# Background sums spaced otherwise, five ordinary tiles ahead of the seven-product groups, and relu with its transposes one step back

## The chip, the cores and the metric

The kernel runs on one core of a Trainium2 chip. The time is device microseconds of one execution, lower is better; what is compared is the median of several executions. The engines are named as the profile names them: PE is TensorE (matmul), PEld its weight load, DVE is VectorE, ACT is ScalarE, POOL is GpSimd, and SP is SyncE, which only issues transfers here. Each engine takes its instructions in the order in which they were written; an instruction that waits holds up all that is queued behind it on its engine.

## The reference

One decoder layer on 256 tokens of width 2048, all in float32:

```
h = rmsnorm(x);  proj = h @ w_in                      # 2048 x 4160
a_out = dilated sliding-window attention, 8 heads     # on the first 3072 columns
b_out = latent attention, 8 heads                     # w_uq, w_ukv
x = x + rmsnorm(concat(a_out, b_out) @ w_out)
h = rmsnorm(x)
u = square(relu(h @ w_up))                            # 2048 x 8192
x = x + rmsnorm(u @ w_down)                           # 8192 x 2048
```

The change lies in the product with `w_up` (the up product), and in transfers that prepare it in the background.

## The kernel before

Stages run one after another: the product with `w_in` and the first attention (to about 190 us of the profiled execution), the latent attention (to about 260), the product with `w_out` (to about 374), the up product (374 to 742), the product with `w_down` (to the end). Weights come as tiles of 128 rows by 1024 columns (512 KB). SP issues the load of a tile into one of five `raw` buffers; ACT rounds it to a first part `hi` (line 308, or 312 where the norm's gain is multiplied in), DVE takes the rest `lo` (line 309 or 313), each into one of eight buffers that are free again when PE has used the tile. A product is then three matmuls of 128x512: hi by hi, lo by hi, hi by lo.

The up product has eight chunks j of 1024 columns. A chunk holds four 128x512 accumulators, for two halves of the tokens and two halves of the columns: half the banks of PSUM, in turn. It walks over sixteen rows of tiles k in two ways. An *ordinary tile* ("k") takes twelve matmuls. A *group* ("w") covers two rows k at once by seven products of half blocks in place of eight, 21 matmuls instead of 24, with sums of weight blocks (right sums) and sums of token blocks (left sums). Three of its products and four others use the four middle banks `m`, which are those that the chunk before has emptied. At a chunk's end the four m banks are combined by ACT and DVE into four tiles c (`close`, lines 1090 and 1093), and DVE adds them onto the accumulators (line 1163). Then the chunk's result leaves: four times ACT makes `r` from an accumulator by relu (line 965), PE transposes r in four pieces into the same bank (`rt`, line 302), and ACT squares that into `uT` (line 978). These steps are spread over the next chunk's first tiles. The next chunk's first group cannot start before the last of them, as it takes those banks for its m.

The right sums of a group come in two ways. *Inline*: POOL fetches two weight tiles into `ab` or `ab2` (line 399), DVE makes the sums t and u (lines 386, 390, 391), and ACT and DVE split them. *Made*: for twelve groups (the table `MADE`), POOL issues transfers from DRAM to DRAM long before (line 368): one copies the two tiles (1024 KB), two add weight blocks onto the copy (512 KB and 256 KB), one adds a block of the copy onto others (512 KB). Each waits for those before it on the same group. They go in batches of `MADE_BATCH` groups: the batch's copies, then its additions, then its last additions.

The order in which each engine's instructions are written comes from a list of steps (`UP_STEPS`) and from chains with a clock of their own (the class `Flow`): each matmul written adds its modelled time to the clock, and a chain's next step is written when the clock has reached its due time. `make_sums` is such a chain: it begins at `D_MADE` and writes one transfer every `MADE_STEP`. `up_evac` is another: `UP_STEP * order` (2.2 each) after it was started it writes the relu, 1.8 later the transposes and the square. These times set only the order of writing. How long something takes on the chip is set by waits.

Of the kernel before, what the change touches and what calls it, by code (L numbers as in the profile page):

```python
# [96 lines left out]


MADE = [(), (1,)] + [(1, 3)] * 5 + [(1,)]
D_MADE, MADE_STEP, MADE_BATCH = 62.0, 4.8, 3  # L100


def up_steps(first, *groups):
    steps = [("k", k) for k in first]
    for i, ks in enumerate(groups):
        steps += [("w", i)] + [("k", k) for k in ks]
    return steps
# [1 line left out]

THREE = up_steps(range(6, 11), (11, 12), (13,), (14, 15))  # L110
FOUR = up_steps(range(8, 12), (12,), (13,), (14,), (15,))
FIVE = up_steps(range(10, 14), (), (14,), (), (), (15,))
UP_STEPS = [up_steps(range(16)), THREE] + [FIVE] * 5 + [FOUR]

ST = 12 * 256
N_SEVEN = [sum(w == "w" for w, _ in steps) for steps in UP_STEPS]
# [149 lines left out]
def layer(nc, tc, io):  # L266
    flow = Flow()
# [12 lines left out]
    def bank(i, name):  # L280
        return ps.tile([P, 512], F32, tag=f"bank{i}", bufs=1, name=name)
# [19 lines left out]
    def transpose(out, a):  # L301
        nc.tensor.transpose(out, a, ident)
        flow.spend(TR)
# [182 lines left out]
    def proj(aT, chs, name, order=None, need=None, bank_of=None):  # L486

        accs = [[[(bank_of or acc_bank)(f"acc_{name}_{c}_{b}_{i}") for i in range(len(ch.cuts))] for b in range(NB)]
                for c, ch in enumerate(chs)]
        order = order or [(0, t, b) for t, b in in_order(len(chs[0].tiles))]  # L490
        left = {(c, b): len(ch.tiles) for c, ch in enumerate(chs) for b in range(NB)}
        uses = {}
        for c, t, b in order:
            ch = chs[c]
            i, k0, kp = ch.tiles[t]
            ws = [weights.get(x) for x in (i if isinstance(i, list) else [i])]
            i = i if isinstance(i, list) else [i]
            if need:
                need(k0 + kp - 1, b)
            if i[0] < FINE:  # L500
                hl = [(0, 0), (1, 0)], [(0, 1)]
            else:
                hl = [(0, 0), (0, 1), (1, 0)],
            for g, passes in enumerate(hl):
                for kk in range(kp):
                    k = k0 + kk
                    for j, (o, m) in enumerate(ch.cuts):
                        wt, o = (ws[j], 0) if len(ws) > 1 else (ws[0], o)
                        for p, (x, w) in enumerate(passes):
                            mm(accs[c][b][j][:, :m], tok(aT[x], k, b), wt[w][:, kk, o:o + m],  # L510
                               k == 0 and g == 0 and p == 0,
                               k == ch.nk - 1 and g == len(hl) - 1 and p == len(passes) - 1, MM * m / 512)
                    flow.pump()
            left[c, b] -= 1
            for x in i:
                uses[x] = uses.get(x, 0) + 1
                if uses[x] == NB:
                    weights.free(x)
            if not left[c, b]:
                yield c, b, accs[c][b]  # L520
# [188 lines left out]
    for half in range(2):  # L709
        qkv = {}  # L710
        for nms in (("qk", "v") if not half else "qkv"):
            accs = [acc for _, _, acc in proj(xT, [ch_a[half, nms]], f"{nms}{half}",
                                              bank_of=at_bank if (half, nms) == (0, "v") else None)]
# [217 lines left out]
    for ns in ((0, 1), (2,), (3,)):  # L931
# [4 lines left out]
        for c, b, acc in proj(mixT, [ch_o[n] for n in ns], f"o{ns[0]}", order, heads_done):  # L936
            n = ns[c]
# [23 lines left out]
    def up_evac(j, b, i, acc, order):  # L961

        yield UP_STEP * order
        r = late["up"].tile([P, 512], F32, tag="r", bufs=2, name=f"r{j}_{b}")
        nc.scalar.activation(r, acc, AF.Relu, scale=rstd2[b])
        yield D_UP if j > 1 else 2 * D_UP
        t = bank(i, f"rt{j}_{b}")
        for k in range(4):
            transpose(t[:, k * P:(k + 1) * P], r[:, k * P:(k + 1) * P])
        if j not in uT:  # L970
            if j < 2:
                t2 = late["u01"][:, j * CW:(j + 1) * CW]
            elif j > 13:
                t2 = late["up"].tile([P, CW], F32, tag="T", bufs=2, name=f"uT{j}")
            else:
                t2 = late["up"].tile([P, CW], F32, tag=f"k{U_HOME.get(j, j)}", bufs=1, name=f"uT{j}")
            uT[j] = t2.rearrange("p (k s) -> p k s", k=4)
        nc.scalar.activation(uT[j][:, :, b * P:(b + 1) * P], t.rearrange("p (k s) -> p k s", k=4), AF.Square)
        if b and 2 <= j < 8:
            flow.start(u_away(j), 6.0)  # L980
# [119 lines left out]
    evac = []  # L1100
    for j in range(FF // CW):
        at = {bn: 4 * (j % 2) + i for i, bn in enumerate(PARTS)}
        if j == 0:
            accs = {bn: acc_bank(f"acc_u0_{bn[0]}{bn[1]}") for bn in at}
            at = {bn: (turn[0] - 3 + i) % 4 for i, bn in enumerate(at)}
        else:
            accs = {bn: bank(i, f"acc_u{j}_{bn[0]}{bn[1]}") for bn, i in at.items()}
        steps = wide_u[j]
        order = in_order(len(steps), (APART[1], 0)) if j == 0 else [(t, b) for t, (w, _, _) in enumerate(steps)
                                                                    for b in range(NB if w == "k" else 1)]  # L1110
        for t, b in order:
            what, k, tiles = steps[t]
            if (j, t, b) == (0, 8, 0):
                flow.finish(*res)
                late["po"].release()
                mix.release()
                late["up"] = pool("up", "right")
                late["st"] = late["up"].tile([P, ST], F32R, tag="st", bufs=1, name="st")
                late["st4"] = late["up"].tile([P, CW], F32R, tag="k2", bufs=1, name="st4")
                for n in ("ab", "ab2", "c", "u01"):  # L1120
                    late[n] = late["up"].tile([P, 2 * CW], F32, name=n)
                flow.start(all_sums())
            if (j, t, b) == (FF // CW - 1, 4, 0):
                weights.limit -= 1
                u_next = split_u(0, 0)
            if (j, what, k, b) == (1, "k", 10, 0):
                more_sums = flow.start(two_sums(), 12.0)
            if (j, what, k) == (1, "w", 2):
                flow.finish(more_sums)
            if (j, t, b) == (FF // CW - 1, 6, 0):  # L1130
                for i in (2, 3):
                    u_back(i, late["up"].tile([P, CW], F32, tag=f"k{i}", bufs=1, name=f"uT{i}_back"))
            if j == 1 and what == "w":
                flow.until(lambda: len(sums) > k)
            if what == "k":
                w = weights.get(tiles[0])
                h_done(k, b)
                for n in range(2):
                    c = slice(n * 512, (n + 1) * 512)
                    three(accs[b, n], [tok(hT[x], k, b) for x in range(2)], [w[x][:, 0, c] for x in range(2)], t == 0, t == len(steps) - 1)  # L1140
                    if j == 0 and t == len(steps) - 1:
                        evac.append(flow.start(up_evac(n, b, at[b, n], accs[b, n], 2 * b + n - 0.25 * (2 * b + n))))
                    flow.pump()
                if b == NB - 1:
                    weights.free(tiles[0])
                continue

            first, last = k == 0, k == N_SEVEN[j] - 1
            if first:
                weights.ahead = W_AHEAD  # L1150
                flow.finish(*evac[-4:])
                m = {n: bank(i, f"m{n}_{j}") for n, i in zip((1, 6, 7, 5), free)}
            blocks = [[tok(hT[x], 2 * k + kk, bb) for x in range(2)] for kk, bb in ((0, 0), (1, 0), (1, 1))]
            if last:
                weights.ahead -= 1
            seven_products(tiles, (blocks, sums[k]), accs, m, first, last, last and N_SEVEN[j] > 3, k in MADE[j])
            if last:
                more = close(closing(), m)
        free = [at[bn] for bn in PARTS]
        if j:  # L1160

            for bn in PARTS:
                nc.vector.tensor_tensor(out=accs[bn], in0=accs[bn], in1=more[bn], op=OP.add)  # L1163
            for o, (b, n) in enumerate(PARTS):
                evac.append(flow.start(up_evac(2 * j + n, b, at[b, n], accs[b, n], o + 0.6)))
    weights.ahead = W_AHEAD
    u_last = evac[-4:]
    up = late["up"]
# [84 lines left out]
    for c in range(2):  # L1253
# [3 lines left out]
        accs = {(b, n): y[b][2 * c + n] for b, n in PARTS}  # L1257
# [107 lines left out]
```

## Time and profile before

| what | us |
|---|---|
| three executions | 1086.21, 1086.35, 1082.34 |
| median | 1086.21 |
| the profiled execution's own time | 1084.39 |
| span of the profiled execution | 1082.6 |
| PE busy in the span | 1042.8 (96%) |
| DVE busy in the span | 836.4 (77%) |
| 16 DMA engines, moved | 273.39 MB, 253 GB/s on the mean |
| mean granted TensorE clock | 0.992 of full speed |

Times inside the profile count from the span's start. A matmul's time in the records overlaps with that of the next one (about 390 ns each, begun about 227 ns apart), so PE's busy share says little by itself; gaps in PE and what ended them say more. Chunks 2 to 6 of the up product, from 470 to 694 us, repeat with a period of 44.6 us, so that one of them stands for five.

### The profile page before, as it was taken

The page shows a single profiled execution, that of the slowest core. Times are in us where ns is not written, and L with a number is a line of the kernel's source. Part 1 is how long each engine was busy: PE and PEld are TensorE (multiplying, and loading weights), DVE is VectorE, ACT ScalarE, POOL GpSimd, SP SyncE. Part 2 cuts the span into 40 slices and gives each one's busy share as a digit, 9 for nine tenths or more (in the row PEclk, how much of TensorE's full clock was granted, in tenths as well). Part 3 has the DMA queues.
Part 4 walks back from the last instruction along what each step waited for, and adds up shares of the span by engine and source line. Part 5 has one row for each costly group of instructions (what it writes and reads, how often), then busy time and mean ns, then how long its engine had stood idle before and what let it go on. Part 6 is the DMA issues. An engine that isn't in the chain of part 4 may idle for free.

```text
span 1082.6 us, 13538 instructions
## 1 busy us (share of the span) xinstructions
PE 1042.8 (96%) x4819; PEld 862.3 (80%) x4819; DVE 836.4 (77%) x1122; ACT 636.5 (59%) x862; POOL 96.0 (9%) x128
## 2 busy tenths in 40 slices
PE   9997899999999999999999999998999999999996
PEld 6886789888788878878778787787888888888885
DVE  6664446566556569889899898897799988999995
ACT  6564345655355466566657557576566655766761
POOL 0022100232101010000000000000000000111100
PEclk9999999999999999999999999999999999999999
DMA  8989967999929476668668585659778767789962
GB/s 299 355 286 259 314 178 227 236 276 323 269 97 302 159 269 246 216 202 280 218 230 273 186 282 190 219 201 390 250 253 293 284 241 263 271 286 315 372 206 85
DMA packets 96692, 273.39 MB, mean 253 GB/s; under 512 B 8304, under 2 KB 12912, under 8 KB 96240
## 3 DMA queue, kind: packets, MB, share of 16 engines
q1 hardware_dynamic: 70624, 190.35, 51.1%
q0 software_dynamic: 25568, 81.80, 25.4%
q8 instruction: 38, 0.62, 0.2%
q10 hardware_dynamic: 432, 0.37, 0.1%
q14 instruction: 30, 0.25, 0.1%
HBM read 253.61 MB, written 47.19 MB: 278 GB/s over the span
## 4 chain that ended last, share of the span: by engine, by line
PE 57%; DVE 21%; DMA 12%; issue 5%; ACT 4%; POOL 0%; DVEq 0%; POOLq 0%; ACTq 0%; SPq 0%
PE y L298 24%; DVE lo L309 9%; DMA raw<-in_w_in 8%; PE acc_o L298 7%; PE acc_u L298 7%; PE md L298 5%; DVE lo L313 4%; DMA raw<-in_w_out 3%; PE acc_ckv L298 2%; ACT hi L308 2%; PE acc_cq L298 2%; PE acc_v L298 2%; DVE t L386 2%; DVE acc_u L1163 1%; PE acc_ukv L298 1%
## 5 line engine op out<-in xcount | busy, mean ns | idle before, releaser
L309 DVE TENSOR_TENSOR lo<-raw,hi 128x1024 fp32r<-128x1024 f32 (+3 forms) x261 | 292.0, 1139 | 145.8 <-ACT hi L308 145.2
L308 ACT ACTIVATE hi<-raw 128x1024 fp32r<-128x1024 f32 (+3 forms) x261 | 253.7, 990 | 161.7 <-DMA raw<-in_w_in 60.4
L298 PE MATMUL y<-hi,uhi 128*128 128x512 f32 x370 | 144.8, 391 | 0.0
L298 PE MATMUL y<-lo,uhi 128*128 128x512 f32 x370 | 144.3, 390 | 0.0
L298 PE MATMUL y<-hi,ulo 128*128 128x512 f32 x370 | 144.2, 390 | 0.0
L298 PE MATMUL acc_u<-hi,hT_hi 128*128 128x512 f32 x320 | 128.3, 401 | 1.5 <-DVE c L1093 1.5
L298 PE MATMUL acc_u<-hi,hT_lo 128*128 128x512 f32 x320 | 125.2, 391 | 0.4 <-DVE hT_lo L309 0.4
L298 PE MATMUL acc_u<-lo,hT_hi 128*128 128x512 f32 x320 | 124.8, 390 | 0.0
L313 DVE SCALAR_TENSOR_TENSOR lo<-raw,gcol,hi 128x1024 fp32r<-128x1024 f32 x62 | 77.2, 1278 | 13.0 <-ACT hi L312 13.0
L298 PEld LDWEIGHTS y<-lo,uhi 128*128 128x128 f32 x370 | 69.7, 188 | 14.5
L298 PEld LDWEIGHTS y<-hi,uhi 128*128 128x128 f32 x370 | 69.8, 189 | 14.4
L298 PEld LDWEIGHTS y<-hi,ulo 128*128 128x128 f32 x370 | 69.7, 188 | 14.4
L312 ACT ACTIVATE hi<-raw,gcol 128x1024 fp32r<-128x1024 f32 x62 | 69.6, 1145 | 13.3 <-DMA raw<-in_w_up 9.3
L298 PEld LDWEIGHTS acc_u<-hi,hT_hi 128*128 128x128 f32 x320 | 60.1, 188 | 14.9 <-DVE c L1093 3.6
L298 PEld LDWEIGHTS acc_u<-hi,hT_lo 128*128 128x128 f32 x320 | 60.0, 188 | 13.8 <-DVE hT_lo L309 0.9
L298 PEld LDWEIGHTS acc_u<-lo,hT_hi 128*128 128x128 f32 x320 | 60.2, 188 | 11.3
L308 ACT ACTIVATE hi<-u 128x1024 fp32r<-128x1024 f32 (+1 forms) x32 | 31.1, 977 | 44.4 <-DVE u L391 32.7
L309 DVE TENSOR_TENSOR lo<-st_down,hi 128x1024 fp32r<-128x1024 f32 x42 | 50.4, 1219 | 3.0 <-ACT hi L308 2.8
L298 PE MATMUL acc_o<-hi,mixT_hi 128*128 128x512 f32 x128 | 52.3, 409 | 0.0
L298 PE MATMUL m<-hi,st 128*128 128x512 f32 x138 | 51.9, 389 | 0.0
L308 ACT ACTIVATE hi<-st_down 128x1024 fp32r<-128x1024 f32 x42 | 43.9, 1052 | 12.5 <-PE y L298 9.5
L298 PE MATMUL acc_o<-hi,mixT_lo 128*128 128x512 f32 x128 | 50.6, 396 | 0.0
(331 smaller groups left out, 2137.1 us busy)
## 6 DMA issues: line engine op xcount, KB each, us to landing
raw<-in_w_down SPq DMA_DIRECT2D x86, 512.0 KB, 5.7
raw<-in_w_up SPq DMA_DIRECT2D x76, 512.0 KB, 5.0
raw<-in_w_in SPq DMA_DIRECT2D x55, 512.0 KB, 6.4
ab<-in_w_up POOLq DMA_DIRECT2D x19, 1024.0 KB, 7.2
raw<-in_w_out SPq DMA_DIRECT2D x32, 512.0 KB, 9.6
made<-in_w_up POOLq DMA_DIRECT2D x12, 1024.0 KB, 14.4
raw<-made SPq DMA_DIRECT2D x24, 512.0 KB, 5.1
ab_down<-in_w_down POOLq DMA_DIRECT2D x11, 1024.0 KB, 7.5
```

The costliest lines, as they stand in the source:

```text
L298: nc.tensor.matmul(out, a, b, start=start, stop=stop)
L308: nc.scalar.activation(hi, src, AF.Copy)
L309: nc.vector.tensor_tensor(out=lo, in0=src, in1=hi.bitcast(F32), op=OP.subtract)
L312: nc.scalar.activation(hi, src, AF.Copy, scale=g)
L313: nc.vector.scalar_tensor_tensor(out=lo, in0=src, scalar=g, in1=hi.bitcast(F32), op0=OP.mult, op1=OP.subtract)
L386: tt(out=two[0], in0=two[1][:, 0:2, :], in1=two[1][:, 1:4:2, :], op=OP.add)
L1163: nc.vector.tensor_tensor(out=accs[bn], in0=accs[bn], in1=more[bn], op=OP.add)
```

## The change

Three tables or constants are altered; no arithmetic is added or removed.

```diff
-D_MADE, MADE_STEP, MADE_BATCH = 62.0, 4.8, 3
+D_MADE, MADE_STEP, MADE_BATCH = 50.0, 8.0, 2
...
-FIVE = up_steps(range(10, 14), (), (14,), (), (), (15,))
+FIVE = up_steps(range(10, 15), (), (), (), (), (15,))
 UP_STEPS = [up_steps(range(16)), THREE] + [FIVE] * 5 + [FOUR]
...
-                evac.append(flow.start(up_evac(2 * j + n, b, at[b, n], accs[b, n], o + 0.6)))
+                evac.append(flow.start(up_evac(2 * j + n, b, at[b, n], accs[b, n], o + (1.6 if N_SEVEN[min(j + 1, 7)] > 4 else 0.6))))
```

The background transfers are written from 50 on instead of 62, one every 8.0 instead of 4.8, in batches of two groups instead of three. Chunks 2 to 6 (`FIVE`) go through rows 10 to 14 as ordinary tiles, then five groups, then row 15; before, row 14 stood between the second and the third group. At the five boundaries in front of these chunks the relu, the transposes and the square are written one step of 2.2 later.

Both places at a boundary, from chunk 2 to chunk 3. On ACT before, behind the copy of the first m bank (`r4`, `r5`: the relu of chunk 2's left and right half of columns, `_0` and `_1` the halves of tokens; 189 to 192 are the tiles of chunk 3's first group, 193 to 196 of its second):

```order
L308 ACTIVATE hi190_4510<-ab2_3564 128x1024
L965 ACTIVATE r4_0_4526<-acc_u2_00_4119,rstd_pre20_3404 128x512
L308 ACTIVATE hi191_4528<-u3_0_4506 128x1024
L965 ACTIVATE r5_0_4541<-acc_u2_01_4120,rstd_pre20_3404 128x512
L978 ACTIVATE uT4_4548<-rt4_0_4543 128x4x128
L308 ACTIVATE hi192_4553<-t3_0_4505 128x1024
L978 ACTIVATE uT5_4568<-rt5_0_4563 128x4x128
L965 ACTIVATE r4_1_4570<-acc_u2_10_4121,rstd_pre21_3499 128x512
L965 ACTIVATE r5_1_4578<-acc_u2_11_4122,rstd_pre21_3499 128x512
L308 ACTIVATE hi193_4582<-raw193_4580 128x512
L978 ACTIVATE uT4_4548<-rt4_1_4589 128x4x128
L978 ACTIVATE uT5_4568<-rt5_1_4601 128x4x128
```

And on ACT now (189 is row 14, 190 to 193 are the first group, 194 to 197 the second):

```order
L965 ACTIVATE r4_0_4541<-acc_u2_00_4117,rstd_pre20_3391 128x512
L308 ACTIVATE hi192_4546<-u3_0_4524 128x1024
L978 ACTIVATE uT4_4561<-rt4_0_4556 128x4x128
L965 ACTIVATE r5_0_4563<-acc_u2_01_4118,rstd_pre20_3391 128x512
L308 ACTIVATE hi193_4571<-t3_0_4523 128x1024
L965 ACTIVATE r4_1_4578<-acc_u2_10_4119,rstd_pre21_3487 128x512
L978 ACTIVATE uT5_4585<-rt5_0_4580 128x4x128
L978 ACTIVATE uT4_4561<-rt4_1_4596 128x4x128
L965 ACTIVATE r5_1_4602<-acc_u2_11_4120,rstd_pre21_3487 128x512
L308 ACTIVATE hi194_4606<-raw194_4604 128x512
L978 ACTIVATE uT5_4585<-rt5_1_4619 128x4x128
L308 ACTIVATE hi195_4634<-raw195_4632 128x1024
```

The relu of the second accumulator still stands behind the split of the sum u, and now also behind the first square; the second group's first split now stands behind the square that waits for the third transposes.

On DVE before, from the last combination of the m banks to the sums of the next group:

```order
L1093 TENSOR_TENSOR c_3565<-m5_2_4231,c_3565 128x512 x2
L309 TENSOR_TENSOR lo189_4482<-ab2_3564,hi189_4481 128x512
L1163 TENSOR_TENSOR acc_u2_00_4119<-acc_u2_00_4119,c_3565 128x512
L1163 TENSOR_TENSOR acc_u2_01_4120<-acc_u2_01_4120,c_3565 128x512
L1163 TENSOR_TENSOR acc_u2_10_4121<-acc_u2_10_4121,c_3565 128x512
L1163 TENSOR_TENSOR acc_u2_11_4122<-acc_u2_11_4122,c_3565 128x512
L386 TENSOR_TENSOR t3_0_4505<-ab2_3564 128x1024
```

And on DVE now:

```order
L1093 TENSOR_TENSOR c_3554<-m5_2_4247,c_3554 128x512 x2
L313 SCALAR_TENSOR_TENSOR lo189_4484<-raw189_4481,gcol_69,hi189_4483 128x1024
L1163 TENSOR_TENSOR acc_u2_00_4117<-acc_u2_00_4117,c_3554 128x512
L1163 TENSOR_TENSOR acc_u2_01_4118<-acc_u2_01_4118,c_3554 128x512
L1163 TENSOR_TENSOR acc_u2_10_4119<-acc_u2_10_4119,c_3554 128x512
L1163 TENSOR_TENSOR acc_u2_11_4120<-acc_u2_11_4120,c_3554 128x512
L309 TENSOR_TENSOR lo190_4508<-ab2_3553,hi190_4507 128x512
L386 TENSOR_TENSOR t3_0_4523<-ab2_3553 128x1024
```

The split of row 14 has come ahead of the four additions onto the accumulators, and the half-wide split that stood there has gone behind them. On PE the four transposes now stand behind the second block of the third tile, the first block of the fourth, the whole fourth tile, and the third block of the fifth; before, behind the third block of the second tile, the second block of the third, the first and the third block of the fourth.

On POOL, behind the norm that ends the product with `w_out`, stood only the fetches for the groups:

```order
L528 TENSOR_TENSOR rstd_pre20_3404<-t_pre20_3403,neg_half_94 128x1
L528 TENSOR_TENSOR rstd_pre21_3499<-t_pre21_3498,neg_half_94 128x1
L399 DMA ab2_3564<-in_w_up 128x2x1024
L399 DMA ab_3563<-in_w_up 128x2x1024
L399 DMA ab2_3564<-in_w_up 128x2x1024
```

Now the last background transfers stand between and ahead of them (`made6_3` is the third group's right sum of chunk 6):

```order
L528 TENSOR_TENSOR rstd_pre21_3487<-t_pre21_3486,neg_half_94 128x1
L368 DMA made6_1_79<-in_w_up 128x2x512
L368 DMA made6_1_79<-in_w_up 128x512
L368 DMA made5_3_78<-made5_3_78 128x2x512
L368 DMA made6_1_79<-made6_1_79 128x2x512
L368 DMA made6_3_80<-in_w_up 256x1x1024
L399 DMA ab2_3553<-in_w_up 128x2x1024
L368 DMA made7_1_81<-in_w_up 256x1x1024
L368 DMA made6_3_80<-in_w_up 128x2x512
L368 DMA made6_3_80<-in_w_up 128x512
L399 DMA ab_3552<-in_w_up 128x2x1024
```

POOL's 48 background transfers stand between its small norm instructions. Ahead of `rstd_kv` (the key and value latent's norm) there were 20 of them before and are 14 now; between `rstd_kv` and `rstd_q`, 5 before and 3 now; between `rstd_q` and `rstd_pw`, 21 before and 13 now; behind `rstd_pw`, 2 before and 18 now.

## The prediction

> **What bounds the kernel now.** I read the page first:
>
> ```profile
> PE 1042.8 (96%) x4819; PEld 862.3 (80%) x4819; DVE 836.4 (77%) x1122; ACT 636.5 (59%) x862; POOL 96.0 (9%) x128
> PE 57%; DVE 21%; DMA 12%; issue 5%; ACT 4%; POOL 0%; DVEq 0%; POOLq 0%; ACTq 0%; SPq 0%
> ```
>
> The matmuls end last nearly everywhere, so only gaps in PE, and stretches where DVE is full, can be won or lost. Next come the busy times by stretch (window, length, busy time of PE, PEld, DVE, ACT, POOL with instruction counts, then granted clock, DMA share, GB/s). First the stretches in which background transfers run, then 342 to 397 (end of the product with `w_out`), 398 to 430 (chunks 0 and 1), and one whole period of the up product.
>
> ```profile
> 80.00:100.00 20.00, 14.85 (x60) 11.39 (x58) 8.18 (x19) 8.82 (x15) 4.34 (x4) 0.91 1.09 252
> 100.00:128.00 28.00, 23.89 (x117) 19.40 (x117) 14.93 (x35) 12.39 (x23) 8.45 (x9) 1.00 1.06 317
> 232.00:260.00 28.00, 25.47 (x132) 22.30 (x131) 16.47 (x39) 13.44 (x28) 5.89 (x7) 0.94 1.09 263
> 260.00:280.00 20.00, 17.91 (x93) 15.31 (x91) 12.19 (x31) 9.96 (x20) 6.19 (x6) 0.91 1.06 334
> 280.00:310.00 30.00, 29.56 (x147) 24.78 (x148) 15.97 (x38) 14.61 (x28) 1.17 (x1) 1.00 0.84 237
> 342.00:397.00 55.00, 54.58 (x256) 44.75 (x255) 34.84 (x51) 27.94 (x47) 4.65 (x6) 1.00 0.60 190
> 398.00:430.00 32.00, 32.00 (x149) 26.53 (x148) 28.09 (x43) 20.32 (x26) 1.51 (x2) 1.00 0.76 283
> 515.30:559.96 44.66, 42.59 (x195) 34.63 (x194) 40.12 (x45) 29.05 (x35) 2.15 (x3) 1.00 0.72 247
> ```
>
> PE idles 5.15, 4.11, 2.53, 2.09 and 0.44 us in the first five rows, 14.3 together; there the transfer engines are full (share above 1). In the period, PE idles 2.07 of 44.66 us and DVE 4.54.
>
> **Part 1: the front.** The queues from 64 to 127 (packets, MB, share of the sixteen engines; q0 carries the background, q1 the weights), the begin of the first background transfers, those behind the two norms, and PE's pace in the latent attention:
>
> ```profile
> q0 software_dynamic: 3976, 10.78, 66.3%
> q1 hardware_dynamic: 4156, 8.01, 38.4%
> ...
> 64.65 2.16 POOL L368 DMA_DIRECT2D made<-in_w_up  x3
> 193.21 0.73 POOL L528 TENSOR_TENSOR rstd_kv<-t_kv,neg_half 128x2 f32<-128x2 f32 x1 [66.06 <-DVE t_kv L527]
> 218.83 0.69 POOL L368 DMA_DIRECT2D made<-in_w_up  x1
> ...
> 214.69 2.72 PE acc_ukv L298 x12
> ```
>
> In these 63 us the weights get 8.01 MB, 0.127 MB/us: a tile of 0.524 MB per 4.1 us, while PE uses one (twelve matmuls) in 2.72. The background moves 10.78/63 = 0.171 MB/us and takes 66.3% of 63 us, 3.87 us of all engines per MB. So as long as the background has work, PE falls behind, until the tiles loaded ahead are used up; then it has gaps.
>
> The order, not the clock of the table, sets when the transfers stop: the change leaves 14 transfers, 8192 KB (8.4 MB), ahead of `rstd_kv`, where 20 stood with 12032 KB (12.3 MB). At 0.171 the first burst lasts 49 us in place of 72 and ends near 114 in place of 137. It begins no earlier: POOL's first ones follow an early norm that the change does not touch. Behind `rstd_q` 13 transfers (7168 KB) stand for 21 (11776 KB): 43 us for 70, ending near 262 in place of 289. PE's gaps behind these new ends should close:
>
> ```profile
> 122.00:128.00 6.00, 3.70 (x17) 1.00 1.07 237
> 268.00:275.00 7.00, 6.49 (x33) 1.00 1.07 300
> 275.00:282.00 7.00, 4.98 (x19) 0.76 1.09 259
> ```
>
> (window, length, PE's busy time.) They are 2.30 + 0.51 + 2.02 = 4.83 us. The gaps between 80 and 112 and before 262 stay, as the shares are the same while a burst runs. I take **-4.8**; the bounds are 0, if the gaps only move, and -14.3, if every one closes.
>
> A page's rule bears on this. The Trainium skill, "DMA: Bandwidth & Descriptors", section "Queues, rings and completion order", says that a transfer engine goes in turn through the queue rows that have work, one packet from each. By it a batch of two instead of three would not lighten a burst while it lasts. The 3976 and 4156 packets above agree with equal turns. Who held instead that the load goes with the size of the batch would get a third of 14.3, also -4.8, and two thirds of part 2's price, 2.7: 1088.1 in all.
>
> **Part 2: the transfers that are now late.** Eighteen stand behind `rstd_pw` (341 us), two before. Those written up to 397 are 3840 KB where 1024 KB stood, 2.88 MB more; they meet the row 342 to 397, where 40% of 55 us is free, 22 us of engine time, against 2.88 x 3.87 = 11. So nothing is charged there, and if that cover were gone the price would be 0.38 (worked out below) of 11, 4.2. Behind the last `rstd_pre`, and ahead of the second fetch for a group, stand 4608 KB, 4.72 MB: 18.3 us of engine time. It meets this (queues from 398 to 430, then POOL and DVE around the two fetches, and a weight load's time to landing):
>
> ```profile
> q1 hardware_dynamic: 2250, 7.97, 68.0%
> q0 software_dynamic: 272, 1.05, 8.0%
> ...
> 398.35 0.77 POOL L399 DMA_DIRECT2D ab<-in_w_up  x1 [0.35 <-DMA raw<-in_w_up]
> 429.05 0.74 POOL L399 DMA_DIRECT2D ab<-in_w_up  x1 [29.93 <-DVE lo L309]
> ...
> 441.32 1.22 DVE L386 TENSOR_TENSOR t<-ab 128x1024 f32<-128x1024 f32 x1
> ...
> 470.60 1.21 DVE L386 TENSOR_TENSOR t<-ab 128x1024 f32<-128x1024 f32 x1
> ...
> raw<-in_w_up SPq DMA_DIRECT2D x76, 512.0 KB, 5.0
> ```
>
> The present 76% of 32 us is 24.3 us; with 18.3 more it is 42.6, or 10.6 beyond the stretch. How much of such a lack becomes PE's idle time is taken from the first burst: 72 us x (1 - 2.72/4.12) = 24.5 us of weights lacking cost 9.26 us (80 to 128), 0.38 of it. So **+4.0**, between 0 (tiles loaded ahead absorb it) and +10.6. The fetches themselves have room. On POOL the first stands behind five transfers, two of which wait for a landing, and goes from 398 to some 410, the sums that need it start at 441; the second stands behind additions that wait for a copy, 429 becomes about 432, needed at 470. Norms on POOL now stand behind single issues of about 1 us, well ahead of their readers.
>
> **Part 3: the five boundaries.** The chain of waits across one (start, us, what):
>
> ```profile
> 517.21 0.70 DVE u L391
> 517.99 1.06 ACT hi L308
> 519.05 0.59 ACT r L965
> ...
> 520.33 2.10 PE acc_u L298 x9
> 522.43 0.44 PE rt L302 x4
> 522.87 1.39 PE acc_u L298 x6
> ...
> 524.69 0.70 PE acc_u L298 x3
> ...
> 527.46 1.21 DVE lo L309
> 528.67 1.15 DVE t L386
> ...
> 561.85 0.70 DVE u L391
> ```
>
> It is a loop through ACT, PE and DVE. DVE ends u at 517.91; ACT splits u and only then makes the second `r`; PE waits for that `r`, then does the four transposes with blocks of matmuls between; ACT makes `uT` and splits the second group's tiles; DVE takes the rest and starts the next t at 528.67. That is 10.76 us from u to t. From t to the next end of u, 562.55, it is 33.9 us, and there DVE has almost no pause. 10.8 + 33.9 is the period.
>
> In the changed order row 14's split stands ahead of the four additions to the accumulators, and the 512-wide split that stood there goes behind them but still ahead of t and u. So `r` and u both come later by the length of row 14's split, 1.2. The rows for it (DVE: the split of five such tiles; PE's wait at the transposes; ACT's `uT`):
>
> ```profile
> 548.12 6.06 DVE L313 SCALAR_TENSOR_TENSOR lo<-raw,gcol,hi 128x1024 fp32r<-128x1024 f32 x5
> 519.68 0.66 PE L302 MATMUL rt<-ident,r 128*128 128x128 f32 x4 [1.73 <-ACT r L965]
> 524.73 0.60 ACT L978 ACTIVATE uT<-rt 128x512 f32<-128x512 f32 x1 [1.02 <-PE rt L302]
> ```
>
> The second `r` still stands behind the split of u, now behind a `uT` as well. Counted from the end of u: 0.08 gap + 0.96 split of u + 0.5 `uT` + 0.7 `r` gives the second transposes at 2.25; three blocks of matmuls and four transposes (2.1 + 0.5) give the third at 4.84; 2.51 of blocks and transposes the fourth at 7.35; then 0.64 transposes, 0.5 `uT`, 1.06 split on ACT, 1.14 on DVE: t at 10.7. The same loop time as now, since the blocks moved in front of the transposes are offset by those no longer behind them. But one 1024-wide split of DVE fewer (1.14) fits into the pause; it comes into the full stretch: 33.9 + 1.14 + 10.7 = 45.8, **+1.15 a boundary, +5.8** for five. PE's pause at the second `r` stays at 1.5 to 1.7, for PE reaches it 1.4 later and `r` comes 1.2 to 1.6 later.
>
> Bounds: if the 1.73 us wait vanishes with no new one, -8.7 over five. If row 14's tile comes late (its load is now issued after row 15's splits free a buffer, near 549.4, with 5.0 to land and 1.1 for ACT: 555.5, against a need at 556.9, only 1.4 to spare) by another 1.5 a boundary, +13. I take the middle one, since its rows exist one by one.
>
> **Sum**, against the profiled execution's own time, 1084.39 (span 1082.6; 0.17% under the median): 1084.4 - 4.8 + 4.0 + 5.8 = **1089.4**, 0.3% above the median.
>
> **Rivals.**
> A, the later relu works: PE's wait for `r` goes (1.73 x 5) and DVE catches up inside a chunk. 1084.4 - 4.8 + 4.0 - 8.7 = 1074.9. For it: PE has five ready tiles to do. Against it: DVE pauses only 4.54 us in 44.66, and `r` keeps its place behind u. Chance 0.15.
> B, the spacing is worth more: the gaps of the front close by two thirds (-9.6), late transfers cost nothing, boundaries as in part 3. 1080.6. For it: 14.3 us of gaps lie there. Against it: the shares within a burst. Chance 0.15.
> C, the slower side: the late burst starves chunks 0 and 1 in full, from the point where tiles loaded ahead are used up (the share already is 0.76). 1084.4 - 4.8 + 10.6 + 5.8 = 1096.0. For it: 42.6 us of work for 32. Against it: only 0.38 of such a lack was felt in the first burst. Chance 0.18.
> That the table's spacing does nothing, because norms and waits on POOL gate the transfers anyway, would leave 1084.4 + 5.8 = 1090.2; the counts between the norms speak against it; 0.04.
> The forecast keeps 0.48, with a range of its own from 1085 to 1095.
>
> **How the numbers follow.** About 0.5% is what a measurement of this kernel tells from no change: 1080.8 and 1091.6. Faster: A and half of B, 0.23. Slower: C and a third of the forecast, 0.34. The rest, 0.43, is the same. The range reaches into A and past C: 1076 to 1097.
>
> **What would show it.** Right: periods near 45.8 from chunk 2 on; PE still waiting about 1.5 for the second `r`; PE without gaps at 122 to 128 and 268 to 282; the transfer engines full after 398, with tiles landing 4 us apart. Wrong: a period at or below 44.7 (part 3), gaps at 80 to 112 gone as well (part 1), PE full from 398 to 440 (part 2), or PE waiting for row 14's tile at the chunk's end.

## The result and the profile after

The change takes 1080.23 us (median; 1078.18 to 1082.91) against 1084.03 for the kernel before, run beside it: a ratio of 0.9962 with a 95% interval of 0.9948 to 0.9975. It is faster by 0.4%, where 1089.4, slower by 0.3%, was forecast; the range of 1076 to 1097 held it, the direction was wrong. Both are within the 0.5% that the prediction called no change, but behind the small sum stand large terms.

The profiled execution after took 1082.9 (span 1081.1), at the upper end of its kernel's executions, so that the profiles differ by 1.5 us only. The same norms and fetches on POOL show where time was won and lost. POOL's timeline (start, us, engine, line, operation) of the kernel before:

```profile
340.61 1.63 POOL L528 TENSOR_TENSOR rstd_pw<-t_pw,neg_half 128x2 f32<-128x2 f32 x1 [58.13 <-DVE t_pw L527]
397.45 0.54 POOL L528 TENSOR_TENSOR rstd_pre<-t_pre,neg_half 128x1 f32<-128x1 f32 x1 [10.08 <-DVE t_pre L527]
474.71 0.72 POOL L399 DMA_DIRECT2D ab<-in_w_up  x1 [23.32 <-DVE lo L309]
697.76 0.71 POOL L399 DMA_DIRECT2D ab<-in_w_up  x1 [16.18 <-DVE lo L309]
```

and of the changed kernel:

```profile
181.83 0.72 POOL L528 TENSOR_TENSOR rstd_kv<-t_kv,neg_half 128x2 f32<-128x2 f32 x1 [70.03 <-DVE t_kv L527]
320.46 1.63 POOL L528 TENSOR_TENSOR rstd_pw<-t_pw,neg_half 128x2 f32<-128x2 f32 x1 [73.80 <-DVE t_pw L527]
379.66 0.56 POOL L528 TENSOR_TENSOR rstd_pre<-t_pre,neg_half 128x1 f32<-128x1 f32 x1 [11.38 <-DVE t_pre L527]
466.93 0.75 POOL L399 DMA_DIRECT2D ab<-in_w_up  x1 [23.29 <-DVE lo L309]
696.24 0.71 POOL L399 DMA_DIRECT2D ab<-in_w_up  x1 [16.18 <-DVE lo L309]
```

At `rstd_kv` the changed kernel is 11.4 us ahead (193.21 before), at `rstd_pw` 20.2, at the last `rstd_pre` 17.8, at the fourth fetch for a group (chunk 2 begins there) 7.8, and at the fetch of the last chunk 1.5. So the front gained 20.2, the way from there into chunk 2, with the first of the five boundaries, took 12.4 back, and the rest of the up product 6.3.

The busy times by stretch after, columns as in the prediction:

```profile
80.00:100.00 20.00, 19.92 (x99) 16.51 (x98) 11.51 (x25) 9.23 (x18) 3.70 (x4) 1.00 1.09 279
100.00:128.00 28.00, 28.00 (x130) 23.21 (x130) 15.62 (x30) 15.92 (x26) 4.09 (x4) 1.00 0.98 299
232.00:260.00 28.00, 28.00 (x160) 25.28 (x159) 21.98 (x59) 18.30 (x40) 4.09 (x4) 1.00 1.07 316
260.00:280.00 20.00, 19.81 (x100) 16.38 (x98) 11.17 (x29) 8.39 (x17) 0.00 (x0) 1.00 0.53 176
398.00:430.00 32.00, 23.99 (x106) 19.60 (x105) 22.72 (x34) 18.74 (x25) 5.16 (x6) 0.89 1.06 341
510.20:556.04 45.84, 43.48 (x194) 34.27 (x194) 40.10 (x44) 28.83 (x35) 2.14 (x3) 1.00 0.70 241
```

All but 0.3 us of PE's gaps in these four stretches of the front are gone, those at 80 to 112 too, which the prediction let stay; the granted clock is 1.00 where it was 0.91 to 0.94. From 398 to 430, where PE had no gap, it now lacks 8.0 of 32 us, at a granted clock of 0.89. The period is 45.84.

PE's timeline after, two rows of transposes (in brackets what the engine waited for), and ACT's waits from 376 to 470 (line, releaser: us in total, times, longest):

```profile
412.50 1.11 PE L302 MATMUL rt<-ident,r 128*128 128x128 f32 x4 [8.01 <-ACT r L965]
515.07 0.66 PE L302 MATMUL rt<-ident,r 128*128 128x128 f32 x4 [1.44 <-ACT r L965]
```

```profile
ACT hi L312 <- DMA raw<-in_w_up: 20.0, 9, 5.4
```

The gap at 412 is a wait for `r`, and ACT is late with `r` because the splits ahead of it in its queue wait for weights: 20.0 us in that stretch. The same row of the kernel before:

```profile
ACT hi L312 <- DMA raw<-in_w_up: 6.6, 6, 1.7
```

The queues from 398 to 430 after (packets, MB, share of sixteen engines); the prediction has the same rows of the kernel before, with 7.97 MB of weights at 68.0%:

```profile
q0 software_dynamic: 2179, 6.27, 67.9%
q1 hardware_dynamic: 1326, 4.62, 37.6%
```

The weights' share has fallen to about what it was in front. At a boundary PE's wait for the second `r` is 1.44, about the 1.5 of the prediction.

### The profile page after: what moved, and what is told of

It is laid out like the page before. It is cut to its first block, busy times and chain, and to the rows that moved or that the text cites. A ratio compares the mean times of both kernels' runs of the same rounds, so it can differ in the third digit from the quotient of the medians.

```text
span 1081.1 us, 13538 instructions
## 1 busy us (share of the span) xinstructions
PE 1045.2 (97%) x4819; PEld 860.3 (80%) x4819; DVE 837.9 (77%) x1122; ACT 636.9 (59%) x862; POOL 96.5 (9%) x128
## 4 chain that ended last, share of the span: by engine, by line
PE 67%; DVE 19%; issue 6%; DMA 5%; ACT 3%; DVEq 0%; POOL 0%; POOLq 0%; ACTq 0%; SPq 0%
PE y L298 24%; PE acc_o L298 8%; DVE lo L309 7%; PE md L298 5%; PE acc_qk L298 4%; DVE lo L313 4%; PE acc_v L298 4%; DMA raw<-in_w_up 4%; PE acc_u L298 3%; PE acc_ckv L298 2%; PE acc_ukv L298 2%; PE acc_q L298 2%; PE acc_cq L298 2%; PE acc_k L298 2%; DVE t L386 2%
## 5 line engine op out<-in xcount | busy, mean ns | idle before, releaser
L298 PEld LDWEIGHTS y<-hi,uhi 128*128 128x128 f32 x370 | 69.8, 189 | 14.3
L298 PEld LDWEIGHTS acc_u<-lo,hT_hi 128*128 128x128 f32 x320 | 61.0, 191 | 11.1
```

The costliest lines, as they stand in the source:

```text
L298: nc.tensor.matmul(out, a, b, start=start, stop=stop)
```

## The experiments

Each ratio is to executions of the kernel before taken beside that kernel; their medians lie between 1082.8 and 1085.8 us, and 1084.0 in the first row belongs to the change. Two columns come from POOL's timeline as above: the norm `rstd_pw`, which ends the front, and the time from it to the fourth fetch for a group, which covers the late transfers. The third is the period from chunk 3 to chunk 4. These three are read from one profiled execution each: e2 leaves the front as it was, and its `rstd_pw` still stands 2.7 us later than that of the kernel before, so a difference of some 3 us in the first column says little.

| kernel | `rstd_pw` at | from there to the fourth fetch | period | median | ratio to before (95%) |
|---|---|---|---|---|---|
| before | 340.6 | 134.1 | 44.65 | 1084.0 | |
| the change | 320.5 | 146.5 | 45.85 | 1080.2 | 0.9962 (0.9948 to 0.9975) |
| spacing alone (e1) | 319.6 | 143.7 | 44.64 | 1072.6 | 0.9881 (0.9859 to 0.9902) |
| boundaries alone (e2) | 343.3 | 135.3 | 45.85 | 1091.3 | 1.0051 (1.0030 to 1.0072) |
| batch of two alone (e3) | 319.8 | 134.2 | 44.65 | 1063.1 | 0.9794 (0.9769 to 0.9820) |
| begin and step alone (e4) | 333.4 | 145.2 | 44.65 | 1091.2 | 1.0057 (1.0033 to 1.0080) |
| begin, step, batch of one (e14) | 319.9 | 137.7 | 44.63 | 1068.0 | 0.9840 (0.9818 to 0.9859) |
| spacing, last ones spread (e10) | 320.8 | 140.1 | 44.63 | 1074.3 | 0.9906 (0.9878 to 0.9934) |

**Spacing alone.** The change with the old rows and the old relu.

```diff
-D_MADE, MADE_STEP, MADE_BATCH = 62.0, 4.8, 3
+D_MADE, MADE_STEP, MADE_BATCH = 50.0, 8.0, 2
```

> Only the table of the background transfers is changed (50, 8.0, batches of 2); rows and relu stay as before. If the three parts add up as the profile of the change reads (front -20.2 by the norm at 340.6 that came at 320.5, late transfers +12.4 between that norm and the fetch at 474.7, boundaries +6.3), this kernel takes 1084.0 - 20.2 + 12.4 = 1076 us, its chunks 2 to 6 keep a period of 44.65, and the wait for r of about 8 us near 412 is there. By the recorded prediction's terms (-4.8 and +4.0) it would take 1083.

1072.6, where 1076 was expected from the profile of the change and 1083 by the terms of the prediction: the whole gain of the front is here, and a late price too.

**Boundaries alone.** The rows of `FIVE` and the later relu, with the old table.

```diff
-FIVE = up_steps(range(10, 14), (), (14,), (), (), (15,))
+FIVE = up_steps(range(10, 15), (), (), (), (), (15,))
...
-                evac.append(flow.start(up_evac(2 * j + n, b, at[b, n], accs[b, n], o + 0.6)))
+                evac.append(flow.start(up_evac(2 * j + n, b, at[b, n], accs[b, n], o + (1.6 if N_SEVEN[min(j + 1, 7)] > 4 else 0.6))))
```

> Only the rows of FIVE and the later relu are changed; the background table stays as before. The recorded prediction's +1.15 per boundary, and the measured period of 45.84 against 44.65, both give 1084.0 + 5.8 to 6.3 = 1090 us, with the front and the up product's first two chunks as before. If the two parts influence each other, the total is other than 1090 by over 2.

1091.3 and a period of 45.85. The prediction's price for the boundaries was right, and this part alone makes the kernel slower. The two differences, -11.9 and +6.8 us, come to -5.1; that of the change is -3.8.

**The table taken apart.** The size of a batch without begin and step, and the reverse.

```diff
-D_MADE, MADE_STEP, MADE_BATCH = 62.0, 4.8, 3
+D_MADE, MADE_STEP, MADE_BATCH = 62.0, 4.8, 2    (e3)
+D_MADE, MADE_STEP, MADE_BATCH = 50.0, 8.0, 3    (e4)
```

> Only MADE_BATCH 3 -> 2; begin 62 and step 4.8 as before, so that 20, 5, 21 and 2 transfers stand between the norms as before. Theory count (the front's gain comes from how many transfers stand ahead of a norm): front as before, the key and value norm at 193, 1084 us. Theory batch (the gain comes from fewer transfers in flight at once, which leaves the weight queue a larger share): the norm near 182, most of the 20 us gained in front, and no late transfers to pay: 1084 - 12 to -20 = 1064 to 1072 us.

> Begin 50 and step 8.0 of the change, batches of 3 as before; 14, 3, 13 and 18 transfers between the norms. Theory count: front gain as in the change, norm at 182 and 320, late price +12: 1076 us. Theory batch: weights' share while a burst runs as before (0.127 MB/us), so that only the ends of the bursts are saved, -4.8, and the late price of 12 stays: 1091 us.

This shows which edit gained the front. The batch of two, with as many transfers ahead of each norm as before, brings the norm `rstd_pw` from 340.6 to 319.8, and the kernel to 1063.1. Begin and step bring it to 333.4 only, 7.2 us earlier in these two profiles. There PE has no gap from 122 to 128 any more, and is still busy for only 3.81 of 6 us from 80 to 86: that is the effect that the prediction worked out, as 4.8. Begin and step then cost 11.1 on the way to the fourth fetch (145.2 against 134.1), so that alone they make the kernel slower.

Why the batch matters is in the queues (packets, MB, share of sixteen engines), from 70 to 74, 74 to 80, 80 to 86 and 92 to 98. The first stretch also has the weight loads that SP issued in it (count, KB each, median us to landing). The kernel before:

```profile
q0 software_dynamic: 377, 1.45, 97.4%
q1 hardware_dynamic: 24, 0.05, 4.0%
raw<-in_w_in SPq DMA_DIRECT2D x4, 512.0 KB, 15.4
...
q0 software_dynamic: 279, 0.92, 53.3%
q1 hardware_dynamic: 487, 0.95, 47.2%
...
q0 software_dynamic: 387, 0.74, 70.0%
q1 hardware_dynamic: 381, 0.73, 39.3%
...
q0 software_dynamic: 386, 0.73, 69.1%
q1 hardware_dynamic: 387, 0.74, 39.4%
```

and the batch of two:

```profile
q0 software_dynamic: 292, 1.11, 75.6%
q1 hardware_dynamic: 152, 0.31, 23.1%
raw<-in_w_in SPq DMA_DIRECT2D x4, 512.0 KB, 7.8
...
q1 hardware_dynamic: 901, 1.73, 77.7%
q0 software_dynamic: 154, 0.33, 27.9%
...
q0 software_dynamic: 404, 0.76, 69.2%
q1 hardware_dynamic: 401, 0.78, 39.3%
...
q1 hardware_dynamic: 636, 1.22, 57.3%
q0 software_dynamic: 293, 0.57, 51.0%
```

The first difference comes ahead of 80. While the first batch's copies run, the weights get almost nothing: from 70 to 74 in the kernel before, four weight loads are issued, and 24 weight packets move against 377 of the background. With two copies instead of three this is over sooner. From 74 to 80 the background then moves little, as POOL had to wait until 73.06 for a copy to land before it issued the first addition, and the weights get 1.73 MB; in the kernel before, where the third copy is still under way, they get 0.95. This decides PE's first gap: in the kernel before ACT waits 6.62 us for a tile, until 80.22, and PE is busy for 3.75 of 6 us from 80 to 86; with the batch of two PE has no gap there.

From 80 to 86 both look alike: equal packets, 39% for the weights. From 92 to 98 the batch of two has fewer background packets, since POOL waits for a landing with too little else queued; the weights get 1.22 MB instead of 0.74. In the kernel before the background's share lies between 53 and 71% in each stretch of 6 us from 74 to 134, as another group's transfers are queued while POOL waits for one; with the batch of two it goes from 28 to 87%.

**Batches of one and of four**, begin and step as before.

> Only MADE_BATCH = 1 (begin 62, step 4.8): each group's copy, additions and last addition follow one another, each waiting for the landing of the one before. Theory holes (packets are shared equally while both queues have work, and a small batch helps by running dry while POOL waits for a landing): the background queue runs dry more often; weights' share of the engines from 80 to 100 above the 46.9% of batch 2; PE stays full as with batch 2, so 1063 us, or some us more if POOL's norms get stuck behind these waits. Theory level (the number in flight sets the share at each moment): the same or more in share while transfers are in flight, which can be told apart where the background queue is never empty: there 39 to 40% by the theory of holes, above 45% by the theory of the level.

> Only MADE_BATCH = 4 (begin 62, step 4.8). Theory holes: with batches of three the background queue already is never empty from 80 to 128 (weights 39 to 40%), so four change little there: 39% again, 1084 to 1091 us. Theory level (share falls with each further transfer in flight): 30 to 33% from 80 to 128, and another 10 us or more of gaps: 1095 us or more.

1065.6 (ratio 0.9833, 0.9809 to 0.9856) and 1085.1 (1.0019, 1.0005 to 1.0034). The queues from 80 to 100 with batches of four, then of one:

```profile
q0 software_dynamic: 1304, 2.68, 69.4%
q1 hardware_dynamic: 1305, 2.51, 39.0%
```

```profile
q1 hardware_dynamic: 1962, 3.79, 54.5%
q0 software_dynamic: 802, 2.04, 42.9%
```

Four change little against three, as the queue was already hardly ever empty: 39.0% for the weights, 39.6% with three. So the share does not fall with each transfer in flight. One lets the queue run dry more often (54.5%, against 46.9% with two), at no further gain, for PE has no gap from 80 to 128 with either.

**The late price.** Two ways to lessen it, on the change's begin and step with the old boundaries: the last sixteen transfers twice as far apart (e10), and batches of one (e14).

```diff
-                    yield MADE_STEP
+                    yield MADE_STEP if i < 8 else 2 * MADE_STEP    (e10, with 50.0, 8.0, 2)
...
+D_MADE, MADE_STEP, MADE_BATCH = 50.0, 8.0, 1    (e14)
```

> The change's background table (50, 8.0, batches of two), old rows and relu, but the last sixteen transfers every 16.0 instead of 8.0, so that fewer of them stand between the last norms of the product with w_out and the first two fetches, and more in chunks 2 to 5. The spacing alone cost 9.5 us there (1072.6 against 1063.1). Theory crowding (the price is paid because 4608 KB meet the weights of chunks 0 and 1 while the transfer engines are full): about half the bytes there, price 0 to 4, total 1063 to 1067 us. Theory lateness (any transfer in the up product costs, as its engines are busy 72% there): price 9 or more, 1072 us or above.

> Begin 50 and step 8.0 of the change, batches of one, old rows and relu. As many transfers stand late as in the change. Theory holes, late too (what starves chunks 0 and 1 is that several background transfers are queued at once, as in front): with one group at a time the queue runs dry between them, and the late price of 9.5 us falls below 4: 1062 to 1067 us. Rival (the bytes that meet chunks 0 and 1 set the price): 1071 us or more.

Both expectations were missed in part. Between `rstd_pw` and the fourth fetch the price against 134.2 is 9.5 with the spacing alone, 5.9 spread and 3.5 with batches of one. The queues from 380 to 440, with the spacing alone, spread, and then batches of one:

```profile
q1 hardware_dynamic: 3201, 11.42, 50.7%
q0 software_dynamic: 2880, 7.60, 49.1%
```

```profile
q1 hardware_dynamic: 3078, 10.97, 51.7%
q0 software_dynamic: 1739, 4.57, 32.5%
```

```profile
q1 hardware_dynamic: 3379, 12.08, 53.0%
q0 software_dynamic: 2733, 7.85, 48.7%
```

About the same bytes cost 9.5 in batches of two and 3.5 in batches of one, and the fewer bytes of the spread kernel cost 5.9, so the price doesn't go by the bytes alone. (With batches of three it is 11.1, e4 against the kernel before.) Batches of one bring a part of it back, and 4.9 us (1068.0 against 1063.1) stay, of which 1.6 fall into chunk 2, whose own period is 46.2. Spread, the kernel is at 1074.3, no better than e1, as one boundary near 590 lost another 4.9 us (577.03 to 599.66 between two fetches, 17.8 at other boundaries). ACT waited 3.66 us there for a weight tile (at 579.54), 12 us after POOL had issued two background transfers; this was not followed further.

**The boundary taken apart**, on the batch of two: the rows alone (e5), the later relu alone (e6), and on the old rows a relu that is 0.6 of a step earlier (e9).

> On the version with only the batch of two (1063.1 us, period of chunks 2 to 6 44.65): FIVE takes row 14 among its ordinary tiles, the relu stays where it was. In this order the second r stands ahead of the split of u on ACT. Theory A (the loop from u through r, the transposes and the next splits sets the period): PE's wait for the second r, 1.4 to 1.7, goes; 33.9 + 1.14 for row 14's split + about 9 = 44.0, 0.6 less a boundary, total 1060 us. Theory B (row 14's split in the full stretch costs its 1.15 whatever the relu does): period 45.8, total 1069 us.

> On the version with only the batch of two: the relu and transposes one step later, FIVE as before. The first r now stands behind the split of u, the second behind the split of t and a square. Theory A: the loop gets longer, as two r instead of one wait for u and the transposes follow later: the fourth transposes come 1 to 2 us later after u, period 45.7 to 46.7, total 1068 to 1073 us. Theory B (the later relu finds PE supplied, so PE's 1.7 us pause goes): period 43, total 1055 us.

> On the version with only the batch of two (1063.1 us, period 44.65), old rows: the relu and transposes 0.6 of a step earlier, so that the second r stands ahead of the split of u on ACT; nothing else moves. Theory (what a boundary costs is decided by how many r stand behind the split of u: one of them 1.4 to 1.8 us of PE's time, two of them 3.5): PE's wait for r nearly goes, period 43.0 to 43.6, total 1056 to 1059 us. Rival (DVE's work alone sets the period, 40.1 of 44.65 busy, and the pause only moves): 44.5, 1062 us.

The medians are 1055.9 (ratio 0.9748, 0.9728 to 0.9768), 1078.3 (0.9950, 0.9930 to 0.9970) and 1056.9 (0.9739, 0.9718 to 0.9760), from 1063.1 with the batch alone. One period of the rows alone, then of the later relu alone, and PE's waits at the transposes of the latter:

```profile
456.35:499.42 43.07, 42.24 (x193) 34.71 (x193) 40.05 (x44) 29.71 (x36) 2.15 (x3) 1.00 0.75 256
```

```profile
503.91:551.17 47.26, 43.17 (x193) 34.39 (x193) 40.11 (x44) 29.03 (x36) 2.14 (x4) 1.00 0.69 234
...
504.25 0.65 PE L302 MATMUL rt<-ident,r 128*128 128x128 f32 x4 [2.24 <-ACT r L965]
...
511.21 0.66 PE L302 MATMUL rt<-ident,r 128*128 128x128 f32 x4 [1.26 <-ACT r L965]
```

The rows gain 1.58 a period, more than either expectation, and the later relu costs 2.61, more than the 1.0 to 2.0 expected; with both, the period is 45.84. DVE's timeline of the rows alone shows where:

```profile
497.29 0.69 DVE L391 TENSOR_TENSOR u<-u,ab 128x512 f32<-128x512 f32 x1
...
506.01 1.22 DVE L386 TENSOR_TENSOR t<-ab 128x1024 f32<-128x1024 f32 x1
```

The way from the end of u to the next t is 8.03 here, against 10.76 before. The rest of the period is 35.04, which is 33.9 and the 1.14 for row 14's split: this term of the prediction is measured. In the order of the rows alone the second `r` stands ahead of ACT's split of u, and so is ready when PE comes; the later relu puts it behind again and the way back to 10.74. The earlier relu on the old rows tests this: it brings the same `r` ahead of u without moving a row, and the period is 43.26, as expected. With the rows alone PE still waits 0.89 for the third `r`, which stands behind the split of u.

**An earlier relu on the new rows**, by 0.4 (e11) and 0.8 (e12) of a step.

```diff
-                evac.append(flow.start(up_evac(2 * j + n, b, at[b, n], accs[b, n], o + 0.6)))
+                evac.append(flow.start(up_evac(2 * j + n, b, at[b, n], accs[b, n], max(o + 0.2, 0.0))))    (e11)
+                evac.append(flow.start(up_evac(2 * j + n, b, at[b, n], accs[b, n], max(o + -0.2, 0.0))))    (e12)
```

> Batch of two and FIVE with row 14 (1055.9 us, period 43.1), relu 0.4 of a step earlier: the third r now stands ahead of the split of u too; only the fourth stands behind it. PE still waits 0.9 a boundary for that third r. Expected: period 42.2 to 42.8, total 1051 to 1054 us. Rival: the wait moves to the fourth r, 43.1 and 1056 us as before.

> As the last one, with the relu earlier still (0.8 of a step): the second r ahead of the split that follows the first. The relu now comes nearer to the additions that it waits for, and ACT's splits behind it start later. Expected: the same as the last within 2 us, 1051 to 1055; rival: r waits for DVE's additions with the splits queued behind it, PE runs out of ordinary tiles, 1058 us or more.

Misses: 1074.3 (ratio 0.9902, 0.9880 to 0.9925) and 1070.0 (0.9856, 0.9836 to 0.9877) in place of 1051 to 1055. A row of ACT's timeline of the first, and its SP queue's:

```profile
512.64 1.06 ACT L308 ACTIVATE hi<-raw 128x1024 fp32r<-128x1024 f32 x1 [4.89 <-DMA raw<-in_w_up]
```

```profile
504.83 0.33 SPq L987 DMA_DIRECT2D uaway<-uT  x1
505.25 0.38 SPq L192 DMA_DIRECT2D raw<-in_w_up  x1
```

The transfer that puts `uT` away is written a fixed time after the square. Moved earlier with the relu, it came to stand ahead of the load of the second group's tile in SP's queue, and that load waited there until `uT` was made. The next kernel (e13) differs from e11 only in that it writes this transfer 6.0 later; e12 was not repeated in this way. The last one (e16) does so too and leaves the relu in front of the last chunk where it was.

```diff
-            flow.start(u_away(j), 6.0)
+            flow.start(u_away(j), 12.0)
...
+                evac.append(flow.start(up_evac(2 * j + n, b, at[b, n], accs[b, n], o + (0.2 if N_SEVEN[min(j + 1, 7)] > 4 else 0.6))))    (e16)
```

> Batch of two, FIVE with row 14, relu 0.4 of a step earlier (1074.3 us, where a weight tile landed 4.9 us late for ACT at two boundaries in a row), and the transfer that puts uT away written 6.0 later, so that on SP the three loads of the next group no longer stand behind its wait for uT. Theory (the loss of that kernel is the load of the second group's tile, issued only when uT was made): the 4.9 us wait goes, period 42.2 to 42.8, total 1051 to 1054 us. Rival (the earlier relu itself disturbs ACT's order): 1070 us or more.

> Batch of two, FIVE with row 14, the relu 0.4 of a step earlier only at the five boundaries in front of chunks 2 to 6, and the transfer that puts uT away 6.0 later. The kernel with the earlier relu at all boundaries had a period near 42.4 against 43.1, and lost 3.5 us in the last two chunks, where the relu is now as before. Expected: 1055.9 - 0.7 x 5 = 1052 us, between 1051 and 1054; rival (the transfer of uT that is now later is what costs there): 1055.9.

1055.9 (ratio 0.9730, 0.9708 to 0.9752) in place of 1051 to 1054, with the period at 42.4 as expected but 3.5 us lost in the last chunk, and then **1052.65** (ratio 0.9699, 0.9661 to 0.9737). This is 3.0% below the kernel before and 2.6% below the change: batches of two at the old begin and step, the new rows, an earlier instead of a later relu.

## Why the prediction was wrong

**Part 1, -4.8 forecast, about -20 measured: the step that failed.** It is the sentence that the gaps between 80 and 112 and before 262 stay, as the shares are the same while a burst runs. The shares are not the same throughout a burst: the first copies leave the weights almost nothing, and later the weights are held to 39% only while the background queue has packets. A batch of two makes that run of copies shorter and lets the queue run dry in between, and it was the batch that brought the gain (e3). How much of it is due to either was not separated. The cut in the number of transfers ahead of a norm, on which the term was built, is worth 7.2 (e4). The rule of the Trainium skill ("DMA: Bandwidth & Descriptors", "Queues, rings and completion order") speaks of queue rows that have work; the rows from 80 to 86 agree with it in both kernels, and what was drawn from it, that a smaller batch would not lighten a burst, was wrong because of that condition. The row from 70 to 74 does not agree with equal turns, 377 packets against 24 with four loads issued, and no run shows why. Which transfers wait for which, and how many others are queued meanwhile, could have been read from POOL's timeline before, and was not used.

The bound of -14.3 was too near as well. It took all idle time of five stretches and left out that PE ran at 0.91, 0.94 and 0.91 of its clock in three of them, in rows that the prediction quotes: on PE's busy time 14.85 x 0.09 + 25.47 x 0.06 + 17.91 x 0.09 = 4.5 us more, an estimate that gives 18.8 in all. PE's records show it too: behind a gap of 2.90 us, that ended at 95.96, matmuls begin 0.43 us apart instead of 0.23 until 98.76.

**Part 2, +4.0 forecast, 9.5 measured.** The place was right, chunks 0 and 1, and the price lies inside the bounds of 0 to 10.6. The term that was mis-sized is 0.38, the part of the lack that PE feels, taken from the first burst: nearly the whole 10.6 was felt. It was too small in front already: `rstd_kv` comes 12.2 us earlier with the batch of two (193.21 to 181.01), half of the 24.5 us reckoned as lacking, where the prediction counted 9.26 of gaps. And the lack itself is not well reckoned from bytes, as the batches of one show (e14). Why more was felt here than in front was not tested; PE's wait at 412.50 is for `r`, which stands on ACT behind splits that wait for weights. The fetches on POOL had room, as worked out.

**Part 3, +5.8 forecast, 6.0 by the periods.** The loop of 10.7, the stretch of 33.9 + 1.14, the period of 45.8 and PE's wait of 1.5 all came as worked out (10.74, 35.1, 45.84, 1.44). What the sum hid is that two edits with opposite signs lie in it. That `r` stands behind the split of u was named as the reason for the wait; the order in which only one of the two edits is made was not looked at.

**The rivals.** B's 1080.6 was met by the number, not by its way: the front gained more than two thirds of its gaps, late transfers did cost, by chance in the same sum. C's price was paid nearly in full (9.5 of 10.6), and the front outweighed it. A fell: PE's wait for `r` stayed. That the spacing does nothing fell as well, since alone it moves the kernel by 11.9 us. Who held that the load goes with the size of the batch had the right constant and a quarter of its gain; four groups instead of three did not lower the weights' share.

## What to carry to other kernels

Ask of a stream of background transfers how often its queue is empty, not only how many bytes it has: one fewer dependent group in flight gave the weights their turns back here, 21 us of 1084. A change that bundles several constants should be priced one constant at a time, since this one held -21, +9.5, -7 and +13 us, which come to -5.5 where -3.8 was measured. Before a chain is moved earlier or later, look for every queue that it writes into; here a store that came too early on SP cost 18.4 us (1074.3 against 1055.9, e11 and e13).

## What had not been expected of the hardware

Equal turns by packet are not equal shares. With both queues busy (80 to 86, kernel before, when the background makes its additions) 387 background packets took 70.0% of sixteen engines for 6 us, 174 ns each, and 381 weight packets 39.3%, 99 ns each, for the same 1.9 KB a packet. So in these rows an addition within DRAM takes 1.8 times the engine time of a load of the same size. A copy does not: from 110 to 116, when copies run, 430 background packets of 3.7 KB took 68.0%, 152 ns each, and 426 weight packets of 1.9 KB took 35.7%, 80 ns each, about 41 ns a KB for both. With equal turns a copy then moves twice the bytes of the loads beside it. And the turns are not always equal: from 70 to 74, during the first copies, it was 377 packets against 24.
